# A decoder trunk whose trace order is planned by an estimate: new figures in the estimate for TensorE's pace, the masked maximum, the Newton steps and the exponential

## The chip, the core and the metric

The kernel runs on one core of a Trainium2 chip, in one launch. The metric is the device time in microseconds (us) of one execution. Five engines take part, each with a queue of its own that it works off in the order in which the program was written: TensorE (PE in the profile, its weight loads PEld), VectorE (DVE), ScalarE (ACT), GpSimd (POOL) and SyncE (SP), which issues the weight transfers.

## The reference

A trunk of two layers for 256 tokens of width 1024, all in float32. Each layer has a half-step SwiGLU, an attention, and another half-step SwiGLU; every sub-layer is normalised and modulated by the conditioning c (adaLN).

```python
for l in range(DEPTH):                       # 2
    h = h + 0.5 * gt * swiglu(modulate(rms_norm(h, ...), sh, sc), ffn_w_in[l, 0], ffn_w_out[l, 0])
    u = modulate(rms_norm(h, norm_g[l, 1]), sh, sc)
    if l == 0: y = dilated_mixer(u, ...)     # 16 heads of 64, 3 dilations, merged by their denominators
    else:      y = nsa_mixer(u, *shared, ...)  # compressed, selected and window branch, 2 key/value heads
    h = h + gt * y
    h = h + 0.5 * gt * swiglu(modulate(rms_norm(h, ...), sh, sc), ffn_w_in[l, 1], ffn_w_out[l, 1])
    if l == 0: shared = shared_kv(h, ...)
```

In both attentions queries and keys are normalised per head (rms_norm) and rotated (rope), and the scores go through a masked softmax.

## The kernel before

Each float32 product is made of three matmuls: a weight is split into a high part `wh` (cast on ACT, L387) and the rest `wl` (subtracted on VectorE, L413), an activation into `uh` and `ul` (for the activations of an FFN L275 and L276), and `mm3` (L466 to L468) adds wh·uh, wl·uh and wh·ul. The attentions' projections do the same with 512 columns (L849 to L851). Weights come in 1 MB pieces from SyncE's queue. The adaLN weights take no matmul; VectorE multiplies and sums them (L393).

The stages follow one another: FFN 0 (with the start to about 215 us), the dilated attention (to about 530 us), FFN 1, FFN 2 with the shared keys and values (to about 970 us), the NSA (to about 1050 us), FFN 3. In the dilated attention four head groups are worked off one after the other, each with three dilations. For each group and dilation a projection leaves queries and keys in PSUM; `qk_task` squares them on ACT (L860), rotates them on VectorE (`rope`, L890, L894, last step on POOL, L895), finds the root's reciprocal from a seed (L877, L879) by three Newton steps on POOL (L581 to L586), scales the result on POOL (L938), and has TensorE transpose it (`transpose4`, L906: four transposes into one PSUM tile `tp`, of which there are two), for each of the two token tiles. The copy out of `tp` is L912 on ACT or L914 on VectorE. A `dil_unit` takes two heads and 128 queries: scores (L967, L969), masked maximum on VectorE (L975), its negative `nb` (L980), exponential on ACT (L983), division (L989, L991), transposes (L906, L912 and L914), products with the values (L1007), and the split of the result (L275, L276).

In the NSA `q_task` (for each of two key/value heads) makes normalised queries (scaling L1329, transposes L1348) and `q_rope` rotated ones (scaling L1329 too); the scores with the compressed keys are L1406; an `nsa_unit` makes scores (L1448), masked maximum (L1455), exponential (L1461), scaling (L1478 on POOL), transposes (L1485) and products (L1504). Copies out of `tp` go to ACT (L1358) or VectorE (L1360).

The order of all this isn't written out. A class `_Clock` keeps an estimate in ns of when each engine is free (`clk.free` for V, A and G, VectorE, ACT and POOL) and of where TensorE stands (`clk.now`). TensorE's bulk matmuls are traced in a fixed sequence, and after each group `tick` moves `clk.now` on; `pump` then lets every task that is due by the estimate trace its next instructions, which is how the transposes and scores get their places among the bulk matmuls. `fill` places the weights' `wl` and the adaLN sums by the same estimate, and `pick` sends a copy or a scaling to the engine that the estimate has done with it first:

```python
    def pick(self, late=0, **cost):
        done = {e: max(self.free[e], self.now) + cost[e] + late * (e == "V") for e in cost}
        e = min(done, key=done.get)
```

Each engine's instructions are held to the order in which they were traced. The estimate runs on the host, when the program is written; the chip sees only the order.

Of the kernel before, what the change touches and what calls it, by code (L numbers as in the profile page):

```python
# [223 lines left out]
class _Kernel:  # L224
# [471 lines left out]
    def products_ahead(self, th, tl, at):  # L696

        w = [self.half(i > 0) for i in range(2)]
        self.ahead_ps = [self.pssc() for _ in range(2)]
        for k in range(KC):  # L700
            for i in range(2):
                j, c = at(k, i)
                c = slice(c, c + P)
                self.mm3(self.ahead_ps[i][:, 0:SX], w[j][0][:, c], w[j][1][:, c], th[:, k], tl[:, k], k == 0,
                         k == KC - 1)
            self.clk.now += 660
            if k + 1 in (FZ, FA, FB):
                yield
# [14 lines left out]
    def ffn(self, u, gate_fn, prep, each=None):  # L723
# [28 lines left out]
        def outer(k, halves):  # L752
            c = slice(k * P, (k + 1) * P)
            for i in halves:
                self.mm3(ps[i // 2][:, (i % 2) * S:(i % 2 + 1) * S], w[i][0][:, c], w[i][1][:, c], uh[k], ul[k],
                         k == 0 and i % 2 == 0, k == KC - 1)
            clk.tick(330 * len(halves))

# [33 lines left out]
        for j in range(j0 + first, NJ):  # L792
            if self.ukv and j == JK:
                clk.finish(self.ukv[1:])
                self.shared_kv(self.ukv[0])
                self.ukv = None
            ps = self.psmm()
            for half in range(2):
                wh, wl = self.half()
                for k in range(KC):  # L800
                    c = slice(k * P, (k + 1) * P)
                    self.mm3(ps[:, half * S:(half + 1) * S], wh[:, c], wl[:, c], uh[k], ul[k], k == 0, k == KC - 1)
                    if k % 4 == 3:
                        clk.tick(330 * 4)
            act(j, ps)
# [5 lines left out]
        for d in range(KC):  # L811
            ps = self.psmm()[:, 0:S]
            for k in range(NJ):
# [9 lines left out]
                if t % 4 == 3:  # L823
                    clk.tick(4 * 330)
            if d == KC - 3 and not early:
# [11 lines left out]
    def projection(self, u, ncols, n, ps):  # L837
# [4 lines left out]
        for b in range(0, KC, n):  # L842
            ws = [self.half(i > 0) if (b + i) % per == 0 else None for i in range(n)]
            for tt in range(TT):
                c = slice(tt * P, (tt + 1) * P)
                for k in range(b, b + n):
# [5 lines left out]
                    if tt == 0 or k < KC - 1:  # L852
                        self.clk.tick(3 * 0.425 * ncols)
                    else:
                        self.clk.now += 3 * 0.425 * ncols
            yield ps
# [100 lines left out]
    def dil_unit(self, hg, hp, qt, oh, ol):  # L957
# [15 lines left out]
        for e in range(2):  # L973
# [3 lines left out]
            sts.append(st)  # L977
            T = clk.V(512, clk.now)
        nb = self.small(2, "nb")
        nc.vector.tensor_scalar(out=nb, in0=mx, scalar1=-SCALE, scalar2=None, op0=ALU.mult)  # L980
        T = clk.on("V", 70, T)
        for e in range(2):
            nc.scalar.activation(out=sts[e], in_=sts[e], func=AF.Exp, bias=nb[:, e:e + 1], scale=SCALE,  # L983
                                 accum_out=den[:, e:e + 1])
            T = clk.A(640, T)
        yield T
# [30 lines left out]
    def out_proj(self, oh, ol, gate_fn, prep, early):  # L1017
# [4 lines left out]
        def part(ps, w, k0, k1):  # L1022
            for k in range(k0, k1):
# [3 lines left out]
                self.mm3(ps, w[0][:, c], w[1][:, c], oh[k], ol[k], k == 0, k == KC - 1)  # L1027
                clk.tick(330)

# [209 lines left out]
    def compress(self, u):  # L1239
# [11 lines left out]
        for i in range(4):  # L1251
# [3 lines left out]
            for k in range(KC):  # L1255
                c = slice(k * P, (k + 1) * P)
                self.mm3(pc, wh[:, c], wl[:, c], uh[k], ul[k], k == 0, k == KC - 1)
                if k % 4 == 3:
                    clk.tick(1320)
                if k == 3:  # L1260
# [16 lines left out]
    def nsa_gates(self, u):  # L1277
# [3 lines left out]
        for k in range(KC):  # L1281
            o = slice(k * P, (k + 1) * P)
            self.mm3(ps, wh[:, o], wl[:, o], u[0][k], u[1][k], k == 0, k == KC - 1)
        self.clk.tick(2640)
        self.gts = self.cp.tile([P, TT, 3, NH], F32, name="gts")
# [17 lines left out]
    def q_task(self, kv, ps):  # L1303
# [28 lines left out]
        for tt in range(TT):  # L1332
            clk.spawn(self.q_rope(kv, tt, ps[tt], qr, st, read, scaled), RL)
        yield "G", 3200.0
        st["rs"] = self.head_newton(x, y, 16)
# [100 lines left out]
    def nsa_unit(self, kv, pr, qt, oh, ol):  # L1436
# [5 lines left out]
        blocks = [(e, b, slice(b * n, (b + 1) * n), b * 2 + e) for e in range(2) for b in range(2)]  # L1442
        yield "P", 3.33 * n, {"sc": 2, "u": 1}
        scs = []
        for e in range(2):
# [4 lines left out]
            scs.append(sc)  # L1450
        yield "V", 4 * (1.04 * n + 70) + 200, {}, {"sc": 2}
        mx, den = self.small(4, "mx4"), self.small(4, "den4")
# [407 lines left out]
```

## Time and profile before

| | before |
|---|---|
| time, median of 3 runs (lowest to highest) | 1270.3 us (1269.4 to 1272.64) |
| time of the profiled execution | 1271.57 us |
| its span | 1269.5 us |
| TensorE, VectorE, ACT, POOL busy | 1211.3, 981.9, 644.7, 265.3 us |
| mean granted clock of TensorE | 0.985 |

The span runs from the first to the last instruction in the trace; the time of the same execution is 2.1 us longer. The granted clock is a share of full speed.

### The profile page before, as it was taken

What the parts mean: (1) busy time and instruction counts of PE and PEld (TensorE: products, weight loads), DVE (VectorE), ACT (ScalarE), POOL (GpSimd) and SP (SyncE); (2) the same over time, 40 slices, a digit from 0 to 9 for tenths busy, and PEclk for the clock granted to TensorE, in tenths of its full rate; (3) what the DMA queues carried; (4) which work ended last, traced back from release to release, by engine and by line L of the source; (5) the groups of instructions that cost most, each with busy time, mean ns of one, the idle gap of its engine ahead of it and who ended that gap; (6) DMA issues with size and microseconds to landing.
All of it is one profiled execution on the core that took longest, in us unless ns stands there. A gap on an engine that the chain in (4) does not pass through costs nothing.

```text
span 1269.5 us, 23369 instructions
## 1 busy us (share of the span) xinstructions
PE 1211.3 (95%) x9373; PEld 1134.9 (89%) x9373; DVE 981.9 (77%) x1743; ACT 644.7 (51%) x1126; POOL 265.3 (21%) x356
## 2 busy tenths in 40 slices
PE   4899999989999999999999999999999889999998
PEld 3899999867787787899999999999998769999998
DVE  6798887885768788688888878778877997777652
ACT  4545454544445444555445456545445587645431
POOL 4480000291544628010000100030001342000000
PEclk9899999998999999999999999999999899999999
DMA  8889887463353645137888847767873004466650
GB/s 320 308 294 334 331 312 298 156 269 140 139 226 133 232 153 212 67 136 285 314 339 334 338 153 272 290 234 302 344 264 133 35 2 163 158 251 246 241 188 17
DMA packets 42733, 284.50 MB, mean 224 GB/s; under 512 B 5249, under 2 KB 6273, under 8 KB 9346
## 3 DMA queue, kind: packets, MB, share of 16 engines
q1 hardware_dynamic: 42626, 283.02, 59.9%
q8 instruction: 73, 1.20, 0.4%
q14 instruction: 34, 0.28, 0.1%
HBM read 281.96 MB, written 1.05 MB: 223 GB/s over the span
## 4 chain that ended last, share of the span: by engine, by line
PE 73%; DVE 14%; POOL 5%; ACT 4%; issue 2%; DMA 1%; SPq 0%; ACTq 0%; DVEq 0%; POOLq 0%
PE mm L466 18%; PE mm L467 18%; PE mm L468 18%; PE mm L849 3%; DVE wl L413 3%; PE mm L850 3%; PE mm L851 3%; DVE st L393 2%; PE tp L906 1%; PE o L1007 1%; DVE y L1455 1%; POOL y L938 1%; POOL rs_t L581 1%; PE sc L967 1%; POOL rs_t L584 1%
## 5 line engine op out<-in xcount | busy, mean ns | idle before, releaser
L413 DVE TENSOR_TENSOR wl<-st,wh 128x1024 fp32r<-128x1024 f32 x361 | 439.0, 1243 | 77.6 <-ACT wh L387 77.3
L387 ACT CAST wh<-st 128x1024 fp32r<-128x1024 f32 x361 | 368.9, 1048 | 133.0 <-PE mm L468 48.8
L466 PE MATMUL mm<-uh,wh 128*128 128x256 f32 x1304 | 364.0, 279 | 1.4 <-DVE y L738 1.4
L467 PE MATMUL mm<-uh,wl 128*128 128x256 f32 x1304 | 364.0, 279 | 1.0 <-DVE wl L413 1.0
L468 PE MATMUL mm<-ul,wh 128*128 128x256 f32 x1304 | 363.7, 279 | 0.0
L466 PEld LDWEIGHTS mm<-uh,wh 128*128 128x128 f32 x1304 | 245.1, 188 | 1.7 <-DVE y L738 1.6
L467 PEld LDWEIGHTS mm<-uh,wl 128*128 128x128 f32 x1304 | 245.1, 188 | 1.5 <-DVE wl L413 1.4
L468 PEld LDWEIGHTS mm<-ul,wh 128*128 128x128 f32 x1304 | 245.1, 188 | 0.0
L466 PE MATMUL mm<-y,wh 128*128 128x256 f32 x832 | 233.5, 281 | 0.1
L467 PE MATMUL mm<-y,wl 128*128 128x256 f32 x832 | 232.3, 279 | 0.0
L468 PE MATMUL mm<-y,wh 128*128 128x256 f32 x832 | 232.2, 279 | 0.0
L393 DVE CUSTOM_DVE_ANT_0 st<-st,cact 128x1024 f32<-128x1024 f32 x152 | 186.0, 1254 | 0.0
L466 PEld LDWEIGHTS mm<-y,wh 128*128 128x128 f32 x832 | 156.4, 188 | 1.5 <-issue 0.9
L468 PEld LDWEIGHTS mm<-y,wh 128*128 128x128 f32 x832 | 156.4, 188 | 0.2 <-DVE y L276 0.2
L467 PEld LDWEIGHTS mm<-y,wl 128*128 128x128 f32 x832 | 156.4, 188 | 0.0
L849 PE MATMUL mm<-wh,uh 128*128 128x512 f32 (+1 forms) x336 | 133.4, 397 | 0.0
L850 PE MATMUL mm<-wl,uh 128*128 128x512 f32 (+1 forms) x336 | 129.1, 384 | 0.0
L851 PE MATMUL mm<-wh,ul 128*128 128x512 f32 (+1 forms) x336 | 128.7, 383 | 0.0
L524 POOL TENSOR_TENSOR y<-y 128x256 f32<-128x256 f32 x20 | 22.8, 1140 | 350.4 <-ACT y L505 350.4
L895 POOL TENSOR_TENSOR y<-y 128x512 f32<-128x512 f32 (+1 forms) x26 | 32.1, 1249 | 235.3 <-DVE y L894 224.2
L849 PEld LDWEIGHTS mm<-wh,uh 128*128 128x128 f32 x336 | 64.3, 191 | 14.3 <-issue 1.8
L275 ACT CAST y<-y 128x256 fp32r<-128x256 f32 x88 | 35.8, 406 | 80.2 <-DVE y L738 78.4
(254 smaller groups left out, 1667.7 us busy)
## 6 DMA issues: line engine op xcount, KB each, us to landing
st<-w_in SPq DMA_DIRECT2D x88, 1024.0 KB, 5.3
st<-w_ada SPq DMA_DIRECT2D x76, 1024.0 KB, 5.5
st<-w_out SPq DMA_DIRECT2D x44, 1024.0 KB, 6.3
st<-w_qk SPq DMA_DIRECT2D x24, 1024.0 KB, 4.8
st<-w_va SPq DMA_DIRECT2D x8, 1024.0 KB, 4.7
st<-w_o SPq DMA_DIRECT2D x8, 1024.0 KB, 5.0
st<-w_vb SPq DMA_DIRECT2D x4, 1024.0 KB, 5.0
st<-w_q SPq DMA_DIRECT2D x4, 1024.0 KB, 6.8
```

The costliest lines, as they stand in the source:

```text
L275: self.nc.scalar.copy(out=hi, in_=src)
L387: nc.scalar.copy(out=wh, in_=src)
L393: nc.vector.tensor_tensor_reduce(out=src, in0=src, in1=self.cact, scale=1.0, scalar=0.0, op0=ALU.mult, op1=ALU.add, accum_out=self.mod[:, ...
L413: (self.nc.gpsimd if eng == "G" else self.nc.vector).tensor_tensor(out=o, in0=src[:, c], in1=i.bitcast(F32), op=ALU.subtract)
L466: mm(out=out, lhsT=ah, rhs=bh, start=start, stop=False, **kw)
L467: mm(out=out, lhsT=al, rhs=bh, start=False, stop=False, **kw)
L468: mm(out=out, lhsT=ah, rhs=bl, start=False, stop=stop, **kw)
L524: self.nc.gpsimd.tensor_tensor(out=self.acc, in0=self.acc, in1=self.sq, op=ALU.add)
L849: mm(out=ps[tt], lhsT=uh[k][:, c], rhs=wh[:, o], start=k == 0, stop=False)
L850: mm(out=ps[tt], lhsT=uh[k][:, c], rhs=wl[:, o], start=False, stop=False)
L851: mm(out=ps[tt], lhsT=ul[k][:, c], rhs=wh[:, o], start=False, stop=k == KC - 1)
L895: (eng or nc.gpsimd).tensor_tensor(out=A, in0=A, in1=B, op=ALU.add)
```

## The change

Some figures of the estimate get other values; no instruction, tile or transfer is added or taken out. A group of three 256-column matmuls counts 350 ns in place of 330 (and its multiples), a column of a projection's matmul 0.4545 in place of 0.425, the dilated unit's masked maximum 680 in place of 602 (`clk.V(512)` is 1.04 · 512 + 70), its exponential 700 in place of 640, since `clk.A(640)`, which is 0.83 · 640 + 60 = 591, gives way to `clk.on("A", 700)`, the NSA queries' Newton steps 4400 in place of 3200, an NSA unit's scores 3.64 in place of 3.33 per key, and its four maxima 4 · (1.04n + 150) + 350 in place of 4 · (1.04n + 70) + 200.

```diff
@@ each FFN, projections, output products: seven such lines, 330, 660, 1320 and 2640 become 350, 700, 1400 and 2800
-            clk.tick(330 * len(halves))
+            clk.tick(350 * len(halves))
@@ proj
-                        self.clk.tick(3 * 0.425 * ncols)
+                        self.clk.tick(3 * 0.4545 * ncols)
                     else:
-                        self.clk.now += 3 * 0.425 * ncols
+                        self.clk.now += 3 * 0.4545 * ncols
@@ dil_unit
-            T = clk.V(512, clk.now)
+            T = clk.on("V", 680, clk.now)
...
-            T = clk.A(640, T)
+            T = clk.on("A", 700, T)
@@ q_task
-        yield "G", 3200.0
+        yield "G", 4400.0
@@ nsa_unit
-        yield "P", 3.33 * n, {"sc": 2, "u": 1}
+        yield "P", 3.64 * n, {"sc": 2, "u": 1}
...
-        yield "V", 4 * (1.04 * n + 70) + 200, {}, {"sc": 2}
+        yield "V", 4 * (1.04 * n + 150) + 350, {}, {"sc": 2}
```

What this moves is seen in the order of the instructions on each engine. In the whole program SyncE's queue stays as it was, row for row.

TensorE, in the fourth head group of the dilated attention, at the place where the transposes of its first dilation stand (the eight of L906 that write `tp` from queries and keys; the other eight of L906 belong to a unit of the third group). Before:

```order
L851 MATMUL mm<-wh,ul 128x512
L906 MATMUL tp<-ident,y 128x128 x8
L967 MATMUL sc<-y 128x256
L969 MATMUL sc<-y 128x128 x2
L967 MATMUL sc<-y 128x256
L969 MATMUL sc<-y 128x128 x2
L906 MATMUL tp<-ident,y 128x128 x8
L1007 MATMUL o<-y 64x128 x8
L849 MATMUL mm<-wh,uh 128x512
```

And now:

```order
L851 MATMUL mm<-wh,ul 128x512
L967 MATMUL sc<-y 128x256
L969 MATMUL sc<-y 128x128 x2
L967 MATMUL sc<-y 128x256
L969 MATMUL sc<-y 128x128 x2
L906 MATMUL tp<-ident,y 128x128 x16
L849 MATMUL mm<-wh,uh 128x512
L850 MATMUL mm<-wl,uh 128x512
L851 MATMUL mm<-wh,ul 128x512
L1007 MATMUL o<-y 64x128 x8
```

The next unit's scores have moved ahead of the eight transposes of the unit before it, so that sixteen transposes stand in one row; the output products have moved behind one group of the projection.

VectorE at the same place: the maxima of the unit whose scores moved (L975, L980) and the copy out of `tp` (L914). Before:

```order
L413 TENSOR_TENSOR wl<-st,wh 128x1024 x2
L914 COPY y<-tp 128x512
L975 ISA y,mx<-sc,shareB 128x512
L975 ISA mx 128x1
L975 ISA y,mx<-sc,shareB 128x512
L975 ISA mx 128x1
L980 TENSOR_SCALAR nb<-mx 128x2
```

And now:

```order
L413 TENSOR_TENSOR wl<-st,wh 128x1024
L975 ISA y,mx<-sc,shareB 128x512
L975 ISA mx 128x1
L975 ISA y,mx<-sc,shareB 128x512
L975 ISA mx 128x1
L980 TENSOR_SCALAR nb<-mx 128x2
L914 COPY y<-tp 128x512
```

The copy went behind the maxima, as on ACT the copy L912 went behind the two exponentials L983 of the same unit.

VectorE in the third head group, between the seed of its second dilation (L879) and the rope of its third (L890 with `shareC`). Before:

```order
L989 RECIPROCAL rd<-den 128x2
L991 TENSOR_SCALAR y<-y,rd 128x512 x2
L413 TENSOR_TENSOR wl<-st,wh 128x1024 x2
L914 COPY y<-tp 128x512
L413 TENSOR_TENSOR wl<-st,wh 128x1024 x2
L276 TENSOR_TENSOR y<-o,y 128x256
L393 ISA st,mod<-st,cact 128x1024
L393 ISA mod 128x1
L393 ISA st,mod<-st,cact 128x1024
L393 ISA mod 128x1
L890 TENSOR_TENSOR y<-mm,shareC 128x512
```

And now:

```order
L914 COPY y<-tp 128x512
L413 TENSOR_TENSOR wl<-st,wh 128x1024 x2
L276 TENSOR_TENSOR y<-o,y 128x256
L393 ISA st,mod<-st,cact 128x1024
L393 ISA mod 128x1
L413 TENSOR_TENSOR wl<-st,wh 128x1024
L393 ISA st,mod<-st,cact 128x1024
L393 ISA mod 128x1
L413 TENSOR_TENSOR wl<-st,wh 128x1024
L890 TENSOR_TENSOR y<-mm,shareC 128x512
```

The reciprocal and the two scalings (L989, L991) have left this stretch for one ahead of the seed; four L413 and two L393 are there as before, in another mix. In TensorE's order the transposes of this third dilation stand three and a half groups of three 512-column matmuls earlier than before, those of the fourth group's third dilation two such groups earlier, those of the third group's second dilation one group earlier; of the second group's third dilation they stand where they stood, with one more L413 on VectorE ahead of its rope. In the NSA POOL's three scalings L1329 are VectorE's now, seven of VectorE's ten copies L1360 of 128x512 are ACT's (L1358), and twelve of the units' transposes L1485 that stood ahead of the first L1348 of the second key/value head stand behind it. In FFN 0 one L413 that stood behind an activation's L738 and L276 stands ahead of them.

## Rows read from the trace of the kernel before

**Rows 1.** The page's part 1: busy us, share of the span, instructions:

```profile
PE 1211.3 (95%) x9373; PEld 1134.9 (89%) x9373; DVE 981.9 (77%) x1743; ACT 644.7 (51%) x1126; POOL 265.3 (21%) x356
```

**Rows 2.** Busy time by stretch (us): each engine's busy us and count, clock, DMA share, GB/s:

```profile
330.00:440.00 110.00, 106.55 (x624) 86.73 (x624) 86.88 (x143) 54.49 (x98) 61.15 (x80) 0.99 0.54 200
560.00:820.00 260.00, 259.99 (x2227) 259.72 (x2225) 217.78 (x340) 139.03 (x209) 6.14 (x5) 1.00 0.76 284
1000.00:1010.00 10.00, 6.16 (x31) 5.38 (x31) 9.39 (x28) 4.78 (x17) 4.81 (x11) 0.57 0.00 1
1010.00:1050.00 40.00, 34.16 (x341) 28.36 (x341) 37.19 (x168) 31.27 (x120) 19.99 (x24) 0.98 0.01 2
```

**Rows 3.** TensorE's waits: us in total, times, longest:

```profile
PE tp L906 <- POOL y L938: 10.3, 8, 3.4
...
PE tp L1348 <- DVE y L1329: 3.3, 1, 3.3
...
PE tp L906 <- ACT y L912: 2.2, 1, 2.2
...
PE mm L467 <- DVE wl L413: 1.0, 1, 1.0
```

**Rows 4.** Busy time by stretch: around three pauses of the dilated stage:

```profile
286.70:296.90 10.20, 9.48 (x31) 7.32 (x32) 2.41 (x8) 5.00 (x11) 1.32 (x2) 0.56 0.20 82
327.70:331.10 3.40, 2.54 (x11) 2.15 (x11) 1.47 (x4) 2.21 (x8) 0.00 (x0) 0.67 0.54 157
436.00:439.40 3.40, 3.20 (x23) 2.79 (x24) 1.23 (x1) 1.30 (x4) 0.15 (x1) 1.00 0.83 306
```

**Rows 5.** TensorE's timeline, 463 to 472 us: start, duration, instruction, idle before:

```profile
468.16 1.03 PE L906 MATMUL tp<-ident,y 128*128 128x128 f32 x8
...
470.74 1.09 PE L906 MATMUL tp<-ident,y 128*128 128x128 f32 x8
```

**Rows 6.** TensorE's timeline, 322 to 329 us:

```profile
323.65 0.70 PE L967 MATMUL sc<-y 64*128 64x256 f32 x2
...
325.26 1.09 PE L906 MATMUL tp<-ident,y 128*128 128x128 f32 x8
328.56 1.23 PE L906 MATMUL tp<-ident,y 128*128 128x128 f32 x6 [2.21 <-ACT y L912]
```

**Rows 7.** ACT's timeline, 322 to 329 us:

```profile
326.43 0.72 ACT L983 ACTIVATE y<-y,nb 128x512 f32<-128x512 f32 x1 [4.74 <-DVE nb L980]
...
327.86 0.56 ACT L912 COPY y<-tp 128x512 f32<-128x512 f32 x1
```

**Rows 8.** TensorE's timeline, second halves of three third dilations:

```profile
363.46 0.65 PE L906 MATMUL tp<-ident,y 128*128 128x128 f32 x4 [1.03 <-POOL y L938]
...
436.20 0.55 PE L906 MATMUL tp<-ident,y 128*128 128x128 f32 x3 [1.33 <-POOL y L938]
...
505.07 0.44 PE L906 MATMUL tp<-ident,y 128*128 128x128 f32 x2 [1.30 <-POOL y L938]
```

**Rows 9.** VectorE's timeline, 349 to 411 us:

```profile
351.43 2.38 DVE L413 TENSOR_TENSOR wl<-st,wh 128x1024 fp32r<-128x1024 f32 x2
...
360.82 3.67 DVE L413 TENSOR_TENSOR wl<-st,wh 128x1024 fp32r<-128x1024 f32 x2 [2.40 <-ACT wh L387]
...
409.50 0.88 DVE L991 TENSOR_SCALAR y<-y,rd 128x512 f32<-128x512 f32 x2
```

**Rows 10.** POOL's timeline, Newton steps, 345 to 364 us:

```profile
357.43 1.08 POOL L584 TENSOR_TENSOR rs_t<-rs_t,qkx 128x16 f32<-128x16 f32 x1
...
358.89 0.22 POOL L586 TENSOR_TENSOR rs_y<-rs_t,rs_y 128x16 f32<-128x16 f32 x1
```

**Rows 11.** Groups by line, 970 to 1050 us: busy us, mean ns, idle before:

```profile
L1360 DVE COPY y<-tp 128x512 f32<-128x512 f32 x9 | 6.0, 680 | 0.0
...
L1358 ACT COPY y<-tp 128x512 f32<-128x512 f32 x11 | 6.2, 578 | 4.2 <-PE tp L1485 4.2
...
L1329 POOL TENSOR_TENSOR y<-y,rs_y 128x512 f32<-128x512 f32 x3 | 3.1, 1043 | 4.8 <-DVE y L895 4.7
```

More of the change, by code (lines that the diff above doesn't have):

```diff
@@ L705, in products_ahead @@
                          k == KC - 1)
-            self.clk.now += 660
+            self.clk.now += 700
             if k + 1 in (FZ, FA, FB):
@@ L803, in ffn @@
                     if k % 4 == 3:
-                        clk.tick(330 * 4)
+                        clk.tick(350 * 4)
             act(j, ps)
@@ L823, in ffn @@
                 if t % 4 == 3:
-                    clk.tick(4 * 330)
+                    clk.tick(4 * 350)
             if d == KC - 3 and not early:
@@ L1027, in part @@
                 self.mm3(ps, w[0][:, c], w[1][:, c], oh[k], ol[k], k == 0, k == KC - 1)
-                clk.tick(330)
+                clk.tick(350)
         for d in range(3):
@@ L1258, in compress @@
                 if k % 4 == 3:
-                    clk.tick(1320)
+                    clk.tick(1400)
                 if k == 3:
@@ L1283, in nsa_gates @@
             self.mm3(ps, wh[:, o], wl[:, o], u[0][k], u[1][k], k == 0, k == KC - 1)
-        self.clk.tick(2640)
+        self.clk.tick(2800)
         self.gts = self.cp.tile([P, TT, 3, NH], F32, name="gts")
```

## The prediction, made before the changed kernel had run

> **What bounds the kernel now.** The page's first part comes first: TensorE is busy 95% of the span, VectorE 77% [rows 1]. That average hides two kinds of stages, so the next view is busy time by stretch [rows 2]. In the FFNs TensorE is never idle: 2227 matmuls of 256 columns in 259.99 us are 0.1167 us each, so 0.350 us for a group of three, and 0.70 us for a group of three with 512 columns. No order can shorten such a stretch. The estimate said 330 ns a group and now says 350, which is right there, and changes nothing by itself. The dilated stage (330 to 440 us: 106.55 of 110) and the NSA (1010 to 1050 us: 34.16 of 40, and 6.16 in the 10 us ahead of it) are where TensorE waits, and only there and at the stages' seams can a new order gain or lose. The list of TensorE's waits says for whom [rows 3]: eight times for POOL's scaled queries and keys (L938), 10.3 us in all, once for ACT's copy L912 (2.2 us), once for the NSA's normalised queries (L1348 for L1329, 3.3 us), and once for a weight's low part (L467 for wl, 1.0 us). In the NSA VectorE is busy 37.19 of 40 us: it sets the pace there, not TensorE.
>
> The clock is the second thing to read [rows 4]. The granted clock is 1.00 in most stretches. It fell to 0.56 between 286.7 and 296.9 us and to 0.67 around 328 us, both at a pause of TensorE, the second one of 2.2 us; after a wait of 1.33 us at 436 it stayed 1.00. These shares mix the two levels, 1.2 and 2.4 GHz. At half speed a stretch of 3.4 us costs 1.7 us, the 10.2 us one, at 0.56, about 4.5.
>
> **The change part by part.** No instruction of arithmetic is added. What changes is the order on each engine, and which engine does ten small operations of the NSA. So each site where TensorE waits is costed by when its work comes in TensorE's own queue (its place, in us of matmuls ahead of it) and when its input is ready. I call T(h,g) the eight transposes of the queries and keys of head group h and dilation g. The work ready behind them doesn't overtake, since an engine takes its instructions in order.
>
> T(3,0) is the largest term. Before, its eight transposes stand at 470.74 us and wait for nothing, with eight transposes of a unit, and then the scores of the next, ahead of them [rows 5]. The new order issues those scores first and then sixteen transposes in a row. That same pattern exists once in the trace [rows 6]: scores at 323.65, eight transposes at 325.26, and the next eight only at 328.56, after 2.21 us for L912. ACT shows why [rows 7]: L912, which empties the bank of the first eight, stands behind the next unit's two exponentials, which start only at 326.43. The new ACT order has the same L983 ahead of L912, and VectorE's L975 now also stands ahead of L914. From scores to the second transposes the pattern takes 328.56 - 323.65 = 4.91 us. Scores at 468.16 give T(3,0) at 473.07 in place of 470.74: **+2.3 us**. Lower bound 0, if the second eight find a free bank and don't need L912; upper 4.0, with a stretch of 3.4 us at half clock behind it.
>
> T(1,2), T(2,2) and T(3,2) each already wait for POOL in their second half: 1.03, 1.33 and 1.30 us [rows 8]. A place that comes earlier there is lost whole, since POOL is the later one. T(2,2) comes 3.5 groups of 0.70 us earlier, 2.4 us; against that two scalings (L991), 0.88 us together [rows 9], leave VectorE's queue just ahead of its rope, so POOL may be 0.9 us earlier: between +1.5 and +2.4, I take **+1.8** (lower bound 0, if POOL's Newton steps shorten as well). T(3,2) comes two groups earlier, 1.4 us, with nothing moved out of VectorE's way; behind it the last units' transposes and output products are pushed together as at T(3,0), worth 0 to 1.8 us: **+2.3** between 1.4 and 3.2. T(2,1) comes one group earlier, 0.7 us, and has some slack before POOL's end is late for it: **+0.3**, between 0 and 0.7. The other seven T move together with their input, or not at all: 0, hidden by the same matmuls as before.
>
> T(1,2) keeps its place, but one more L413 stands ahead of its rope on VectorE, 1.19 us of two in 2.38 [rows 9]. Does POOL finish that much later? A POOL step of Newton takes 1.08 us in the stretch in which VectorE runs L413, and 0.22 once VectorE waits for ACT's wh, from 358.4 to 360.8 us [rows 9, 10]. Started 1.15 us later the steps meet one L413 fewer, and gain back one slow step, 0.86 us: **+0.3**, between 0 and 1.15. The Trainium skill says on the page "SBUF — State Buffer" (Who interferes with whom) that a VectorE instruction with two SBUF inputs blocks a GpSimd instruction that reads SBUF, for its whole length. The trace agrees in kind (1.08 against 0.22 us). By that rule the slow steps go with VectorE's L413, and the term is 0.3 as above; by steps of a fixed length, as the planner has them, it is 1.15, and the sum 0.9 us more.
>
> The first FFN: the low part for which L467 waits 1.0 us is issued ahead of the activation's low part (L738, L276) in the new order, so it is ready when TensorE comes to it: **-1.0**, between -1.0 and 0. Other low parts move by one or two L393, each about as long as an L413: 0, since TensorE's own matmuls cover them (such a wait stands once in the whole list). Without that cover each would cost up to 1.2 us.
>
> NSA: VectorE loses seven copies of 0.680 us to ACT (0.578 there) and gets three scalings from POOL (1.043 there), each priced as a copy of the same 512 columns [rows 11]: 4 times 0.680 or 2.7 us less in the stretch that it bounds, while ACT, at 31.27 of 40 us, gets 4.1 more and stays the less loaded. That is the lower bound, -2.7. Against it, twelve transposes of units that before stood ahead of the wait at L1348 (3.3 us) now stand behind it, 1.6 us of work by the eight in 1.09 us [rows 5], which no longer fills TensorE's pause. Were the pause at L1348 paid twice by that, it would cost +3.3, the upper end. VectorE is fuller than TensorE, so I take a value on the side of the gain: **-1.0**. The larger figures for the masked maximum, the exponential and the Newton steps act only through these choices.
>
> Sum: 2.3 + 1.8 + 2.3 + 0.3 + 0.3 - 1.0 - 1.0 = +5.0 us. The profiled execution took 1271.57 us (span 1269.5), so it would take 1276.6; the median of the runs shown is 1.3 us lower, 1270.3, which makes **1275 us**. With all low ends: 0 + 0 + 1.4 + 0 + 0 - 1.0 - 2.7 = -2.3, 1268; with all high: 4.0 + 2.4 + 3.2 + 0.7 + 1.15 + 0 + 3.3 = 14.8, 1285.
>
> **The rivals.** (a) The waits only trade places. T(1,2), T(2,2) and T(3,2) find POOL earlier by as much as they come earlier themselves, because everything ahead of them on ACT and VectorE moves too, and only T(3,0) is paid: 2.3, less 1.0 in the FFN and 1.0 in the NSA, is +0.3, 1270.6, no change. For it: in seven of twelve T the place and the input move together. Against: POOL's end is what is waited for three times in a row at the third dilation, and its start hangs on VectorE's queue.
>
> (b) Faster. Its place is the NSA from 1000 to 1050 us. VectorE's 2.7 us come off in full, and the stretch from 1000 to 1010 us, at clock 0.57 [rows 2], runs at full clock since TensorE's work there is bunched: 6.16 us of busy time at half pace are then some 3 us shorter. With the FFN's 1.0 that is -6.7 us, and the result is 1264 if the dilated stage gives nothing. It decides as soon as the dilated terms stay under 2.9 us, 0.3% being 3.8. Against: L1348 still waits for the same Newton steps, and the pause ahead of it gets longer, so the clock has a reason to fall, not to rise.
>
> (c) Slower still, by the clock: the wait at T(3,0) and the longer ones at T(2,2) and T(3,2) (1.3 + 1.8 and 1.3 + 1.4, both over the 2.2 us of the pause at 328) are followed by half clock as at 287 and 328 us. Two or three such stretches at 1.7 to 4.5 us: 1279 to 1284. Against: the transposes' halves split a wait, and that at 436 us cost no clock. The Trainium skill ("TensorE: Matmul & The Clock Gate", What's actually happening) states that the throttled clock is the default and that activity releases it, so that each longer pause would be paid twice; the rows at 287 and 328 us agree, that at 436 us shows a pause that was free of it.
>
> **How the numbers follow.** Chances: my sum 0.33, (a) 0.27, (b) 0.20, (c) 0.20. A measurement of this kernel can tell about 0.3% (3.8 us) from no change. Slower by more than that are the sum and (c), 0.53; within it (a), 0.27; faster (b), 0.20. The range of 8 in 10 goes from 1265, which takes in the upper part of (b), to 1283, most of (c); the likeliest case has 1272 to 1279 by itself.
>
> **What would show it.** Right: TensorE's list of waits has L906 for ACT's L912 twice, the second at about 473 us and 2 to 3.2 us long; L906 for POOL's L938 rises from 10.3 to some 14 us; L467 for wl is gone; TensorE's pauses in the fourth head group grow by 4 to 5 us; VectorE's L1360 is down to three copies of 512 columns and POOL has no L1329. Wrong: waits at T(2,2) and T(3,2) as before, or a stage from 1000 to 1050 us that is over 3 us shorter; then the step that failed is that POOL's end stays where it was, or that L1348's wait stays.

## The result, and the profile after

The changed kernel takes 1287.5 us (median of four runs, 1282.7 to 1293.7) against 1271.5 for the kernel before: 1.0138 of its time, with a 95% interval of 1.011 to 1.0167. It is 16 us slower, above the range's upper end of 1283. The direction was right, the size three times too small.

The page's part 1 of the changed kernel, from a run of 1293.74 us with a span of 1291.5:

```profile
PE 1222.5 (95%) x9373; PEld 1144.2 (89%) x9373; DVE 977.3 (76%) x1739; ACT 647.6 (50%) x1133; POOL 258.7 (20%) x353
```

The shares are those of [rows 1] within a point: the average says nothing of 16 us. Busy time by stretch does (columns as in [rows 2]):

```profile
330.00:440.00 110.00, 103.87 (x595) 84.72 (x594) 87.22 (x141) 52.73 (x93) 61.71 (x80) 0.98 0.54 199
...
1000.00:1010.00 10.00, 10.00 (x55) 8.34 (x53) 7.28 (x41) 3.86 (x14) 1.18 (x2) 1.00 0.08 32
1010.00:1050.00 40.00, 31.34 (x235) 26.20 (x235) 34.09 (x139) 25.20 (x97) 16.07 (x26) 0.79 0.00 1
```

In 330 to 440 us TensorE gets through 595 instructions where it did 624. The NSA starts some 12 us later here, so its stretch from 1010 to 1050 us answers to 998 to 1038 us of the kernel before:

```profile
998.00:1038.00 40.00, 31.96 (x282) 27.32 (x283) 37.70 (x161) 28.08 (x109) 18.03 (x31) 0.87 0.00 1
```

VectorE is now idle for 5.9 of 40 us where it was idle for 2.3, and the clock is at 0.79 where it was 0.87: VectorE fills the stage less than it did. TensorE's waits, those that answer to [rows 3] and three more:

```profile
PE tp L906 <- POOL y L938: 13.0, 12, 3.4
...
PE tp L906 <- ACT y L912: 6.5, 3, 2.2
PE tp L1348 <- DVE y L1329: 5.7, 1, 5.7
...
PE tp L1142 <- POOL y L1134: 2.9, 1, 2.9
...
PE tp L1389 <- DVE y L1383: 1.9, 1, 1.9
...
PE mm L467 <- DVE wl L413: 1.2, 1, 1.2
...
PE tp L906 <- DVE y L991: 0.5, 1, 0.5
```

These come to some 13 us more than before in the same seven lines (before, the three that [rows 3] doesn't have were 1.7 us at L1142, 0.5 at L1389 and none for L991). The L467 in this list stands at 1069 us, in the NSA's output product; the one of [rows 3], at 101 us, is gone. Beside them stands what the waits do to the clock. Stretches of busy time around six pauses (for three places of the dilated attention, as [rows 4]; then L1142, the NSA's start, its end):

```profile
360.00:366.00 6.00, 3.66 (x19) 3.23 (x18) 2.27 (x3) 2.24 (x5) 3.14 (x2) 0.72 0.74 274
472.00:480.00 8.00, 5.79 (x37) 4.57 (x36) 5.98 (x12) 3.79 (x10) 0.68 (x1) 0.79 0.56 205
526.00:534.00 8.00, 5.64 (x41) 4.82 (x39) 2.59 (x7) 2.76 (x7) 0.00 (x0) 0.79 0.00 0
852.00:858.00 6.00, 3.99 (x21) 3.99 (x22) 2.90 (x5) 2.00 (x4) 2.91 (x6) 0.72 0.73 296
1012.00:1032.00 20.00, 13.51 (x58) 12.15 (x58) 16.51 (x53) 9.26 (x33) 7.20 (x14) 0.57 0.00 0
1066.00:1074.00 8.00, 5.89 (x43) 4.89 (x42) 3.22 (x6) 4.31 (x10) 3.02 (x2) 0.79 0.00 0
```

Length times one less the clock is what a stretch loses, if its matmuls are on the path: 6 times 0.28, or 8 times 0.21, is 1.7 us at each of five places, and 20 times 0.43 is 8.6 at the NSA's start. All five are new: in the trace of before the clock is 1.00 at their counterparts. The one at the NSA's start is not, since from 1000 to 1020 us that trace has 0.74, which is 5.2 us lost; it has grown by 3.4. One at 554 us of the kernel before is gone.

The sixteen transposes in a row, which the prediction costed by a pattern elsewhere. TensorE's timeline and ACT's (start, duration, instruction, idle before):

```profile
470.06 0.70 PE L967 MATMUL sc<-y 64*128 64x256 f32 x2
...
471.67 1.09 PE L906 MATMUL tp<-ident,y 128*128 128x128 f32 x8
474.98 0.78 PE L906 MATMUL tp<-ident,y 128*128 128x128 f32 x4 [2.21 <-ACT y L912]
```

```profile
472.84 0.72 ACT L983 ACTIVATE y<-y,nb 128x512 f32<-128x512 f32 x1 [4.71 <-DVE nb L980]
...
474.27 0.56 ACT L912 COPY y<-tp 128x512 f32<-128x512 f32 x1
```

Scores to second transposes: 474.98 - 470.06 = 4.92 us, against 4.91 in [rows 6], with the same 2.21 us behind ACT. The pattern came again to 0.01 us. It came a second time, at the stage's end:

```profile
529.37 1.48 PE L906 MATMUL tp<-ident,y 128*128 128x128 f32 x8 [2.12 <-ACT y L912]
...
534.70 1.09 PE L1007 MATMUL o<-y 128*64 128x128 f32 x16 [0.93 <-DVE y L276]
```

The third dilations of groups two, three and four, both halves, to be read against [rows 8]:

```profile
361.21 0.66 PE L906 MATMUL tp<-ident,y 128*128 128x128 f32 x4 [1.01 <-POOL y L938]
363.19 0.69 PE L906 MATMUL tp<-ident,y 128*128 128x128 f32 x2 [1.33 <-POOL y L938]
...
433.56 0.66 PE L906 MATMUL tp<-ident,y 128*128 128x128 f32 x4 [0.84 <-POOL y L938]
435.54 0.55 PE L906 MATMUL tp<-ident,y 128*128 128x128 f32 x3 [1.32 <-POOL y L938]
...
508.59 0.66 PE L906 MATMUL tp<-ident,y 128*128 128x128 f32 x4 [0.86 <-POOL y L938]
509.59 0.55 PE L906 MATMUL tp<-ident,y 128*128 128x128 f32 x3 [0.34 <-POOL y L938]
```

T(1,2) waits 2.34 us for 1.03, T(2,2) 2.16 for 1.33, T(3,2) 1.20 for 1.30.

Both programs have the same 7944 weight matmuls (L466 to L468, L849 to L851) in the same sequence, so a trace can be laid against that of before matmul by matmul. How much later than in the trace of before each stage's last one starts, less the same at the stage's first, is the stage's own loss. In us, worked out from the starts in the traces of most of the runs below (the heads are the stages; hg1 to hg4 are the head groups):

```
                FFN0  hg1   hg2   hg3   hg4  FFN1,2  L1142  NSA   FFN3
changed         -1.3 -1.5  +3.8  -0.4  +7.2   +0.7   +2.8  +7.7  +2.3
changed again   -1.1 -3.5  +4.0  -0.4  +7.2   -1.6   +2.5  +7.9  +0.6
dilonly         -1.0 -4.2  +3.9  -0.4  +7.2   -1.4    0.0   0.0  +0.5
nsaonly         -1.3 -3.7  -0.2   0.0  -0.1   +0.1   +0.1  +3.0  +0.1
ffnonly         -1.3 -0.1   0.0   0.0  -0.1   +0.5   +1.2  +1.3   0.0
newt            -1.1 -4.4  -0.2   0.0  -0.1   +2.3   +0.1  +8.5  +1.7
nsaV            -0.4 -1.2  -0.2   0.0  -0.1   +1.8    0.0  +7.5  +0.1
warm            -1.3 -3.5  +4.0  -0.4  +7.3   +0.6   +2.8  +4.3  +0.6
nonsa           -1.3 -1.5  +2.4  +1.2  +7.2   -1.0   +1.2  +3.6  +0.6
a9x             -1.3 -1.1  -1.6  -3.8  +5.6   -1.0   +1.2  +4.9  +0.7
qk9000          +0.4 -3.9  -5.2  -1.2  +4.9   -0.9   +0.1  +1.0  +0.1
b1              -0.3 -3.2  -5.2  -1.2  -0.1   +0.1    0.0   0.0   0.0
```

Each row is one execution, and those of `dilonly`, `nsaonly` and `nonsa` are the fastest of their runs, so the whole differences below are taken from the medians. The columns FFN0 and hg1 carry negative numbers also in runs whose order there is that of before (nsaonly, newt): the trace of before had a wait of 1.0 us at 101 us, which those two don't have, and lost 5.1 us to the clock from 287.9 to 298.2 us (4.5 of them in the window of [rows 4]), where most of the other runs lost 1.7 or 3.4. So hg1 shows no effect of the change, and FFN0 at most a part of one. How hg3 and hg4 share their sum of 6.8 moves by 1.1 us with the matmul at which they are parted. What is missing to a run's whole difference lies at the stages' seams and is under 1.5 us in all.

### The profile page after: what moved, and what is told of

It is laid out like the page before. It is cut to its first block, busy times and chain, and to the rows that moved or that the text cites. A ratio compares the mean times of both kernels' runs of the same rounds, so it can differ in the third digit from the quotient of the medians.

```text
span 1291.5 us, 23411 instructions
## 1 busy us (share of the span) xinstructions
PE 1222.5 (95%) x9373; PEld 1144.2 (89%) x9373; DVE 977.3 (76%) x1739; ACT 647.6 (50%) x1133; POOL 258.7 (20%) x353
## 4 chain that ended last, share of the span: by engine, by line
PE 78%; DVE 10%; POOL 5%; ACT 4%; issue 2%; DMA 1%; SPq 0%; ACTq 0%; DVEq 0%; POOLq 0%
PE mm L466 19%; PE mm L467 18%; PE mm L468 18%; PE mm L849 4%; PE mm L850 3%; PE mm L851 3%; DVE wl L413 3%; DVE st L393 2%; PE tp L906 2%; PE o L1007 1%; PE sc L967 1%; POOL y L938 1%; POOL rs_t L581 1%; POOL rs_t L584 1%; PE sc L466 1%
## 5 line engine op out<-in xcount | busy, mean ns | idle before, releaser
L413 DVE TENSOR_TENSOR wl<-st,wh 128x1024 fp32r<-128x1024 f32 x361 | 438.7, 1242 | 96.3 <-ACT wh L387 95.7
L466 PE MATMUL mm<-uh,wh 128*128 128x256 f32 x1304 | 366.7, 281 | 1.2 <-DVE y L738 1.2
L467 PE MATMUL mm<-uh,wl 128*128 128x256 f32 x1304 | 365.3, 280 | 0.0
L468 PE MATMUL mm<-ul,wh 128*128 128x256 f32 x1304 | 363.3, 279 | 0.0
L466 PEld LDWEIGHTS mm<-uh,wh 128*128 128x128 f32 x1304 | 245.6, 188 | 1.5 <-DVE y L738 1.4
L467 PEld LDWEIGHTS mm<-uh,wl 128*128 128x128 f32 x1304 | 245.9, 189 | 0.0
L468 PEld LDWEIGHTS mm<-ul,wh 128*128 128x128 f32 x1304 | 245.7, 188 | 0.0
L466 PE MATMUL mm<-y,wh 128*128 128x256 f32 x832 | 234.7, 282 | 1.0 <-ACT wh L387 0.9
L467 PE MATMUL mm<-y,wl 128*128 128x256 f32 x832 | 233.0, 280 | 1.2 <-DVE wl L413 1.2
L468 PE MATMUL mm<-y,wh 128*128 128x256 f32 x832 | 231.9, 279 | 0.0
L393 DVE CUSTOM_DVE_ANT_0 st<-st,cact 128x1024 f32<-128x1024 f32 x152 | 185.7, 1252 | 0.0
L466 PEld LDWEIGHTS mm<-y,wh 128*128 128x128 f32 x832 | 156.6, 188 | 2.0 <-ACT wh L387 1.2
L467 PEld LDWEIGHTS mm<-y,wl 128*128 128x128 f32 x832 | 156.7, 188 | 1.4 <-DVE wl L413 1.4
L468 PEld LDWEIGHTS mm<-y,wh 128*128 128x128 f32 x832 | 156.7, 188 | 0.0
L849 PE MATMUL mm<-wh,uh 128*128 128x512 f32 (+1 forms) x336 | 134.1, 399 | 0.0
L851 PE MATMUL mm<-wh,ul 128*128 128x512 f32 (+1 forms) x336 | 129.6, 386 | 0.0
L849 PEld LDWEIGHTS mm<-wh,uh 128*128 128x128 f32 x336 | 64.8, 193 | 14.3 <-issue 1.8
```

Of the source, the lines that this page charges most:

```text
L393: nc.vector.tensor_tensor_reduce(out=src, in0=src, in1=self.cact, scale=1.0, scalar=0.0, op0=ALU.mult, op1=ALU.add, accum_out=self.mod[:, ...
L413: (self.nc.gpsimd if eng == "G" else self.nc.vector).tensor_tensor(out=o, in0=src[:, c], in1=i.bitcast(F32), op=ALU.subtract)
L466: mm(out=out, lhsT=ah, rhs=bh, start=start, stop=False, **kw)
L467: mm(out=out, lhsT=al, rhs=bh, start=False, stop=False, **kw)
L468: mm(out=out, lhsT=ah, rhs=bl, start=False, stop=stop, **kw)
L849: mm(out=ps[tt], lhsT=uh[k][:, c], rhs=wh[:, o], start=k == 0, stop=False)
```

## The experiments

**The changed kernel again, and its stages apart.** `again` is the changed kernel. `dilonly` has the new figures only where they order the dilated attention, `nsaonly` only in the NSA, `ffnonly` only in the feed-forward layers:

```diff
 dilonly: 680 and 700 in dil_unit, 350 for the output product, and
-                        self.clk.tick(3 * 0.425 * ncols)
+                        self.clk.tick(3 * (0.425 if len(self.halves) > 150 else 0.4545) * ncols)
 nsaonly: 4400, 3.64, 150 and 350, 1400, 2800, and
+                        self.clk.tick(3 * (0.4545 if len(self.halves) > 150 else 0.425) * ncols)
 ffnonly, and its multiples:
-            clk.tick(330 * len(halves))
+            clk.tick(350 * len(halves))
```

> The changed kernel once more. Its first four runs lay in two groups, 1282.7 and 1283.8 against 1291.3 and 1293.7 us, and its first trace (1293.74) has a pace of 117.8 ns per matmul of 256 columns in the third feed-forward layer where the kernel before had 116.7 to 117. Sites theory (all of the loss is waits and half-clock stretches at the sites whose order moved): every run near 1291 to 1294, and the same waits. State theory (part of the 16 us is a pace of TensorE that comes and goes between executions): again two groups some 9 us apart, and a trace of the lower group has 116.7 to 117 ns there and some 4 us less in the feed-forward layers.

> Only the figures that order the dilated attention: the projection's 0.4545 there, the masked maximum 680, the exponential 700, the output product's 350; TensorE's order in that stage is then that of the changed kernel, row for row, and that of before elsewhere. Sites theory: +9.5 us against before, 1281. My prediction's sum for this stage: +7.0, 1278. If the loss needs the other stages: under +4.

> Only the figures that order the NSA (projection 0.4545 there, Newton steps 4400, scores 3.64, maxima 150 and 350, the gate's and compression's ticks); the dilated stage and the shared keys and values as before. Sites theory: +7 us, 1278, with a wait of about 5.7 us at L1348 and half clock behind it. My prediction: -1.0, 1269.

> Only the feed-forward layers' 330 to 350 (and 660 to 700). Sites theory: -1.2 us in the first layer for the low part at 101 us, and +3.9 at the shared keys' transposes L1142 (a wait of 2.9 for 1.7 us and half clock behind it): +2.7, 1274. My prediction: -1.0, since I costed L1142 at nothing: 1269.

Measured, all beside 1268.4 for before: `again` 1285.4 us (ratio 1.0133, 1.0114 to 1.0151), `dilonly` 1281.0 (1.0102, 1.0082 to 1.0122), `nsaonly` 1273.6 (1.0040, 1.0020 to 1.0059), `ffnonly` 1271.7 (1.0024, 1.0012 to 1.0037). All four are slower, and the parts' 12.5, 5.2 and 3.3 us make 21 where the whole is 17: more than the whole by about what the three intervals allow; the losses belong to their places. In size the sites theory is near for the dilated stage (9.5 us expected, 10.7 in groups two to four of that trace, 12.5 by the runs). For the NSA it said 7; the runs have 5.2, the trace 3.0. At L1142 it has the wait right, 2.9 us in `ffnonly` as in the changed kernel, but the clock stayed at 1.00 behind it, hence 1.2 and not 2.6. The two groups of runs 9 us apart that the other theory expected didn't come again (1284.6 to 1288.1), but the changed kernel's two traces, of one order, differ by 2.0 us in the first head group, 2.3 in FFN 1 and 2, and 1.7 in FFN 3. My prediction's number for `nsaonly` and `ffnonly`, a gain, was wrong both times.

**One figure of the NSA alone.** `newt` has the queries' Newton steps, `nsaV` the maxima:

```diff
 newt:
-        yield "G", 3200.0
+        yield "G", 4400.0
 nsaV:
-        yield "V", 4 * (1.04 * n + 70) + 200, {}, {"sc": 2}
+        yield "V", 4 * (1.04 * n + 150) + 350, {}, {"sc": 2}
```

> One figure alone: the NSA queries' Newton steps 4400 for 3200, all else as before. In TensorE's order the scores L1448 and products L1504 of other units then stand ahead of L1348 of the second key/value head. Theory that the pause at L1348 sets the NSA's loss: the pause of 3.3 us is filled, the half-clock stretch behind it shrinks by a third or more, 2 to 4 us faster than before. Rival, that each move of this planner's order costs something: 0 to 4 us slower.

> One figure alone: the NSA unit's four maxima, 150 and 350 for 70 and 200. TensorE's order has scores, compressed products and L1504 ahead of L1348 too, and copies go from VectorE to ACT. Pause theory: the pause is filled, 1 to 4 us faster. Rival, that the copies on ACT are what costs 7.8 us in the changed kernel: 4 us or more slower.

Measured beside 1270.3: `newt` 1275.6 (1.0045, 1.003 to 1.0061), `nsaV` 1276.9 (1.0059, 1.0037 to 1.0081). The pause theory fell. The work that moved ahead of L1348 has a wait of its own: L1432, which needs the compressed branch's softmax (L1427). TensorE's timeline, first of `newt`, then of `nsaV`:

```profile
1005.37 0.66 PE L1432 MATMUL tp<-ident,y 128*128 128x128 f32 x2 [7.29 <-DVE y L1427]
```

```profile
1010.70 0.66 PE L1432 MATMUL tp<-ident,y 128*128 128x128 f32 x2 [7.74 <-DVE y L1427]
```

A pause of 3.3 us for L1348 became one of 7.3 and 7.7 for L1432. A Newton time of 4.4 us is about what the trace of before shows (999.17 to 1003.47 us on POOL), and putting it right makes the stage 8.5 us longer by itself in the trace, and the kernel 5.3 by the medians. `nonsa` is the converse: the changed kernel with these three figures put back.

> The changed kernel with the NSA's own three figures (Newton steps 4400, scores 3.64, maxima 150 and 350) put back, TensorE's pace and the dilated unit's figures as changed. If those three figures make the NSA's 7.8 us: 1278, 7 us faster than the changed kernel. If the projection's pace makes it: 1285, no faster.

Measured 1287.0 (beside 1270.1; 1.0135, 1.012 to 1.0151): as slow as the changed kernel, though in its trace, the fastest of its four runs, the NSA loses 3.6 us and not 7.8. So no single figure is the loss's owner: each changed order of this stage, by the pace or by its own figures, is slower than that of before, by 3.0 to 8.5 us in the traces, while `ffnonly` and `qk9000`, which have TensorE's old order there, differ from before by 1.3 and 1.0.

**TensorE kept busy ahead of L1348.** `warm` is the changed kernel, `warmb1` the version `b1` below, each with added matmuls (20 and 12) that nobody reads:

```diff
             tp = self.pst()
+            if kv and tt == 0:
+                for _ in range(20):
+                    nc.tensor.matmul(out=tp, lhsT=self.kT[kv][0][:, 0:P], rhs=self.kT[kv][0], start=True, stop=True)
             for i in range(4):
```

> The changed kernel with 20 matmuls of 512 columns added whose results are thrown away (they are overwritten in the same PSUM tile), just ahead of L1348 of the second key/value head, where TensorE stood 5.67 us: 4.65 us of work at full clock, so nothing waits longer for it. Clock theory (of the NSA's 7.8 us some 4 to 5 are half-clock matmuls behind the pause): the granted clock stays at or near 1.00 from there on, 3 to 5 us faster than the changed kernel, about 1281. Rival (the NSA runs at the pace of the chain from maxima to copies, and TensorE's clock is hidden): less than 1.5 us faster.

> The run with 9000 in three groups (median 1261.95), with 12 matmuls of 512 columns added whose results are thrown away, ahead of L1348 of the second key/value head, where TensorE stood 3.28 us and the granted clock was at half behind it (5.1 us lost between 990 and 1002 us): 2.8 us of work at full clock inside the pause. Clock theory: at least two of the three half-clock stretches of 1.7 us go, and 1 to 3.5 us of the total, 1258.5 to 1261 beside the run without them. Rival (the NSA goes at the pace of the chain from maxima to copies, so that half-clock matmuls there are hidden): within 0.7 us of the run without them.

> The run with 9000 in three groups once more, as the partner of the one with added matmuls on the same chip: 1261 to 1263, 8 us faster than before.

In the trace of `warm` the clock in this stretch goes from 0.57 to 0.91:

```profile
1012.00:1032.00 20.00, 15.45 (x127) 12.91 (x126) 19.02 (x74) 12.80 (x45) 8.31 (x10) 0.91 0.01 1
```

By these shares 6.8 us of matmul time are given back. The added matmuls delay nothing: L1348 starts 7.5 us after the compressed scores L1406 with and without them. The stage is 3.5 us shorter in that trace (+4.3 for +7.8), but the six timed runs, 1282 to 1294, have a median of 1288.3 (beside 1270.3) and show no gain. The other pair, `warmb1`, 1261.7, and `b1again`, 1262.3 (both beside 1269.0), shows no difference. Their stretches from 990 us, `warmb1` first:

```profile
990.00:1002.00 12.00, 11.61 (x58) 9.69 (x57) 11.36 (x40) 5.90 (x21) 5.13 (x13) 0.72 0.00 1
```

```profile
990.00:1002.00 12.00, 8.24 (x41) 7.04 (x41) 11.38 (x37) 6.10 (x20) 5.26 (x14) 0.57 0.00 1
```

Clock 0.72 for 0.57 is 1.8 us of matmul time, and the stage is 0.1 us shorter. VectorE is busy 11.4 of 12 us in both. That would fit the rival, that half-clock matmuls are hidden where VectorE sets the pace, but it doesn't show it. TensorE's timeline, first of `warmb1` (where the added matmuls are L1349 and L1348 has become L1351), then of `b1again`:

```profile
991.89 5.47 PE L1349 MATMUL tp<-shareA 128*128 128x512 f32 x12
997.16 0.74 PE L1351 MATMUL tp<-ident,y 128*128 128x128 f32 x4
```

```profile
994.99 1.09 PE L1348 MATMUL tp<-ident,y 128*128 128x128 f32 x4 [3.26 <-DVE y L1329]
```

The added matmuls ran at half clock themselves, 5.47 us where 2.8 was planned, and held the transposes back by 2.2 us. So a delay and a gain by the clock came together, and the pair can't part them.

**The figure that was left alone.** POOL's Newton steps in the dilated attention stand at 6100 ns in the estimate; in the changed kernel POOL took from 350.32 to 359.11 us for those of T(1,2), 8.8 us. `qk9000` is the kernel before with that figure at 9000, `b1` has it in the first three groups only, `b2` has 12000 for one dilation besides, and `a9x` is the changed kernel with the edit of `b1`:

```diff
 b1:
-        T = clk.on("G", 6100, clk.on("V", 400, T))
+        T = clk.on("G", 9000 if len(self.dil) < 4 else 6100, clk.on("V", 400, T))
```

> The kernel before with one other figure: POOL's Newton steps of the dilated attention, 9000 for 6100 ns (the trace has 8.0 to 10.5 us beside VectorE's weight work). The transposes T then stand 3.5 to 10 us later among the projection's matmuls, where POOL is done, and the sixteen transposes in a row at 325 us are parted. Theory that the dilated stage's loss is the T that come ahead of POOL's end, with half clock behind them: the waits of 3.4, 2.2, 2.2, 1.0, 1.3 and 1.3 us shrink to a third and two or more half-clock stretches of 1.7 us go, 6 to 12 us faster than before, against up to 4 us of fill that is missing at the stage's end. Rival (a moved T costs elsewhere what it saves): within 3 us of before.

> The kernel before with POOL's Newton steps at 9000 ns in the first three head groups and 6100 in the last, so that TensorE's order in the last group is that of before, row for row. In the trace of the run with 9000 throughout, groups one to three gained 9.1 to 10.4 us of the stage and the last lost 4.9. Theory that the loss is the missing fill at the stage's end alone: the 4.9 us come back, 1262, some 8 us faster than before. Rival (the last group's work is late because the stage ahead of it is shorter, so the loss stays): 1267.

> As the run with 9000 in three groups, and 12000 for the second dilation of the first group, where a wait of 5.6 us for POOL was left: its transposes stand twelve matmuls of 512 columns (2.8 us) later. Theory of places (a transpose that comes later waits less by as much): the wait falls to 2.8 us and, with it, the half-clock stretch behind it (1.7 us) may go: 2 to 4 us less than with 9000 in three groups. Rival (POOL's chain of three dilations bounds the first group, so a pause only moves to the third dilation or the units): within 1 us.

> The changed kernel with the figure that it left alone set to what the trace shows too: POOL's Newton steps of the dilated attention 9000 for 6100 in the first three groups. Theory that the change failed there because it made TensorE's pace right and left POOL's too short, so that the transposes moved further ahead of POOL: the second group's 3.9 us come back and more, 9 to 13 us faster than the changed kernel, 1273 to 1277. Rival (the loss is a matter of each order's chance, not of this ratio): less than 5 us.

`qk9000`: 1267.1 (beside 1270.3; 0.9973, 0.9957 to 0.9989), 3.2 us faster, at the edge of the smaller expectation; three groups gain, and the fourth loses 4.9 us, since its last transposes stand behind the last projection matmul with nothing between them. `b1` gives that back: 1262.0 (beside 1270.1; 0.9935, 0.9922 to 0.9947), the 1262 expected, and 8 us faster than before. `b2`, 1262.9, is no better, but it doesn't decide between its two theories, since it moved other transposes than it meant. Those of the second dilation, which stand twelve matmuls later (279.6 us for 277.2), wait for nothing in either run; the long wait, 5.65 us in `b1` and 5.47 in `b2`, is that of the third dilation at 287 us, whose place is the same. `a9x`: 1275.0 (beside 1270.1; 1.0035, 1.0021 to 1.0048), 4.9 us slower than before where `again` is 17.0 slower. TensorE's waits for POOL in its dilated stage fall from 13.0 us in 12 pieces to

```profile
PE tp L906 <- POOL y L938: 7.7, 4, 5.7
```

and the second group, +3.8, is at -1.6.

## Why the prediction was wrong in size

Two steps of the sum failed above all. It set the NSA at -1.0 us, by the argument that VectorE hides TensorE's pause, and the stage lost 7.7 to 7.9. And it put the half clock behind the new waits at nothing, leaving it to rival (c); it came behind those of the dilated stage and at L1142, 1.7 us each time.

**T(3,0), +2.3.** Right to 0.1 us as a wait (2.21 us, same cause, same releaser). But the half-clock stretch behind it, which I had put into the upper bound and into rival (c), came as well: 1.7 us in both traces of the changed kernel (in that of `a9x` the same wait of 2.2 us was free of it).

**T(1,2), +0.3.** The step that failed is "gain back one slow step". POOL's timeline after:

```profile
356.16 1.08 POOL L584 TENSOR_TENSOR rs_t<-rs_t,qkx 128x16 f32<-128x16 f32 x1
357.33 0.20 POOL L585 TENSOR_SCALAR rs_t<-rs_t 128x16 f32<-128x16 f32 x1
...
359.11 4.03 POOL L938 TENSOR_TENSOR y<-y,rs_y 128x512 f32<-128x512 f32 x2
```

Six steps of Newton were slow before, and six are slow after: the weights that VectorE works on moved along with the rope. L938 grew on top of it, from 3.02 us to 4.03, beside two L413. The end I took as the upper bound, 1.15, is what the wait grew by, and a bit more: 1.3; and T(1,1), which I had at 0, stands one group of matmuls earlier and waits 0.8. With a half-clock stretch of 1.7 us the group lost 3.8 to 4.0 us for 0.3. The Trainium skill's rule ("SBUF — State Buffer", Who interferes with whom) agrees with 1.08 against 0.20 us here; what I counted wrong was how many VectorE instructions stand beside POOL's.

**T(2,2) +1.8, T(2,1) +0.3.** T(2,2) grew by 0.8, less than half of the term. A wait of 0.73 us for L912 at 393 us went away and one of 0.5 for L991 at 398 us came, and the third group as a whole lost between nothing and 0.7 (-0.4 in the table), by where it is parted from the fourth. POOL was earlier by most of what the transposes were, so this part of rival (a) held in the main.

**T(3,2) and the tail, +2.3.** T(3,2) itself lost nothing (1.20 for 1.30), the tail the 2.1 us of a second sixteen-transposes pattern and 1.7 us of half clock. The mechanism I named for the tail was right, its price too low.

**FFN 0, -1.0.** Right in kind, at twice the size. None of the six traces with the new order there has the wait at 101 us; of the ten with the old order six have it, 0.4 to 1.5 us long, which makes 0.5 on the average of the ten. I had taken one trace's wait for that of the order.

**L1142, 0.** I hadn't named it. Its transposes moved four groups of three matmuls ahead, the wait went from 1.67 to 2.88 us, and the clock fell behind it: 2.5 to 2.8 us.

**The NSA, -1.0.** The largest error, 8 to 9 us. The step was "VectorE is fuller than TensorE, so I take a value on the side of the gain". The seven copies and three scalings did move as costed (21 copies L1358 of 512 columns on ACT for 14, four scalings of rotated queries on VectorE for one, none on POOL), but TensorE's pauses were not hidden behind VectorE: L1348 waited 5.7 us for 3.3 and L1389 1.9 for 0.5. I had seen that the pause would grow, by 1.6 us of work that no longer fills it, and set VectorE's 2.7 against it; the two waits alone grew by 3.8. How the 7.8 us divide between waits and clock stays open. `nsaonly`, which has the changed kernel's order there up to the output product and the same two waits, lost as much to the clock as before, 5.0 us, and its stage is 3.0 longer; `a9x`, with the same order and waits, lost 8.6 to the clock and is 4.9 longer; the changed kernel lost 8.6 and 1.7 and is 7.7 longer. By these three the loss grows with the clock, but the trace of `warm`, with 3.4 us lost, is 4.3 longer, and the timed runs settle nothing.

**The clock.** Rival (c) had a chance of 0.20 and the right mechanism: pauses of 2.1 to 2.9 us at four places (that of T(1,2) in two parts), each with 1.7 us behind it, and 1.7 us more at the NSA's end. It counted two or three such places in the dilated stage, and none at L1142 or in the NSA. In the row of `again` the five places of the change (hg2, hg3, hg4, L1142, the NSA) make 4.0 - 0.4 + 7.2 + 2.5 + 7.9 = 21.2 us. The other columns make -5.6, most of it clock that the trace of before lost in its first group and at 554 us, at the seam to FFN 1. The sum, 15.6, stands beside 16.4 us between the two spans. So the 16 us measured are some 21 at the places that the forecast was about, where it had 6.0 with nothing for L1142, less what the one trace of before was itself slow.

**Why the change failed in the dilated stage** is shown only in part. The thought that led to `a9x` and `b1` is this: the change made the estimate right about TensorE and left POOL's Newton steps, 8 to 9 us, at 6.1. Before, a TensorE figure that was 6% too short partly made up for that, since transposes due after so many ns come after more matmuls when each counts fewer. With the pace right, the transposes came earlier among the matmuls, ahead of POOL. `a9x` bears this out for a part: with POOL's figure at 9000 in three groups 12 of the 17 us come back. But the same edit also makes the kernel before 8 us faster (`b1`), so beside it the change still costs 13 us (1275.0 for 1262.0). The left-over figure thus accounts for some 4 us of the 17. Between the traces of `a9x` and `b1` the second group still loses 3.6 us, though POOL's figure is 9000 in both, the fourth, where it stayed at 6100, 5.7, and the NSA 4.9. Which of the changed figures puts the sixteen transposes in a row no run has taken apart.

## What to carry to other kernels

An order that is planned by an estimate can get worse when figures of the estimate get better, here by 16 us. So look first for the figure whose waits the profile shows (here POOL's, 10.3 us in the list of waits, and worth 8 us by itself). Price a new wait on TensorE together with the half clock that may follow it: it followed pauses of 2.1 to 2.9 us at four places here, 1.7 us each, but the wait of 2.9 us at L1142 had it behind it in three traces (the changed kernel's two and `warm`) and not in three others (`ffnonly`, `nonsa`, `a9x`). And lay a second trace of the same kernel beside the first before a gain of 1 us in one place goes into a sum.

## What the runs showed that I had not expected

TensorE's pace at a granted clock of 1.00 differs between executions: from 600 to 800 us, all feed-forward matmuls of 256 columns without a wait, TensorE got through these numbers in before, `newt` and the changed kernel's two runs (busy time by stretch):

```profile
600.00:800.00 200.00, 199.99 (x1712) 199.72 (x1712) 166.85 (x260) 105.11 (x158) 6.14 (x5) 1.00 0.79 295
```

```profile
600.00:800.00 200.00, 200.00 (x1698) 199.87 (x1697) 167.33 (x259) 104.08 (x155) 6.14 (x5) 1.00 0.78 287
```

```profile
600.00:800.00 200.00, 200.00 (x1699) 199.93 (x1699) 166.75 (x261) 104.54 (x156) 5.30 (x5) 1.00 0.79 292
```

```profile
600.00:800.00 200.00, 200.00 (x1714) 199.92 (x1714) 168.37 (x262) 103.14 (x156) 5.26 (x5) 1.00 0.78 293
```

The second and third are 0.8% below the others, 1.6 us in 200. `newt` has the kernel's old order here and the changed kernel both speeds, so the order isn't the cause; what is, no run here tells.
